# Three modulation groups moved from the last HGRN2 head to heads 3, 5 and 7

## The chip, the cores and the metric

The kernel runs on one core of a Trainium2 chip. The metric is the device time of one execution in microseconds (us); the kernel before takes 1847.86 us, the median of three runs (1847.52 to 1853.19 us). All times inside an execution are counted from its first instruction.

## The reference

The model has two layers over 512 latent and 256 context tokens of width 1024. Each layer is a token mixer and a SwiGLU FFN, and each of the two is fed by an RMS norm that is scaled and shifted by the layer's modulation, and its output is gated by the modulation.

```python
mod_l = jnp.split((jax.nn.silu(c) @ ada_w[i] + ada_b[i])[:, None, :], N_MOD, axis=-1)
...
x = x + mod_l[2] * o_l
x = x + mod_l[5] * swiglu(modulate(rms_norm(x, norm2_w[i]), mod_l[3], mod_l[4]), ...)
```

Layer 0 mixes with latent attention, layer 1 with HGRN2: eight heads, each a gated linear recurrence over the tokens in both directions. `mod[0]` and `mod[1]` (shift and scale of the mixer) are needed before the heads, `mod[2]` when the mixer's output is added to x, and `mod[3]` to `mod[5]` only in the FFN after it.

## The kernel before, in words

**Modulation groups.** The modulation of a layer is a vector of 6144 = 48 x 128 numbers for the two streams. `ada(l, u0, n, ...)` (line 150) computes n = 4 blocks of 128 of it, called a group here and named by its first block u0: four loads of 512 KB (tile `adaw`, line 155), 32 matmuls with two PE instructions each (line 158) into one PSUM bank, a copy on ACT (line 161, tile `rows`), four transposes (line 164) into a second bank and two small operations on DVE (lines 166 and 168). Groups 24, 28 and 32 of layer 1 are a shift and half of a scale for the FFN of layer 1. They read nothing that the heads make.

**The second layer's heads.** `hgrn` loops over h = 0 to 7 (the text counts heads from 1, so head 8 is h = 7). For each head it writes in this order: `head_proj` (projections by the weights HW for two forget gates, q and the output gate: four weight tiles), for every even h the values `iv` of two heads (two weight tiles HWI), `head` (the recurrence: six levels of small matmuls `lv` on PE, each followed by two multiplications on DVE at line 1060, the `grow` step, and a gather `km` on POOL at line 975; then `u`, state updates on DVE, the outputs `o` and the transposes `otp`), and then the modulation groups that a table gives to this head:

```python
for u in ADA_HG[h]:
    with self.at("ada_g"):
        self.ada(1, u, 4, tmp, self.big)
```

After the last head the output projection follows: `out(n)` adds up eight terms, one per head, with one weight tile HWO per n. Five of these sums (three in the three banks `L`, `L`, `M`, two in the bank group that the levels used) can take the terms of the first seven heads while the last head is at work; their eighth terms wait for its result (`o_hi`, line 590). Group 36 comes after these five.

**How a weight gets to PE.** `weight` (line 72) loads 512 KB into a tile `wf` from SP's queue, ACT copies it to a rounded tile `wh` (line 83), and POOL subtracts to get the rest, `wl` (line 84). PE multiplies with both in every term: lines 97, 98 and 99 are the three products. There are four `wf` buffers, and **the loads `adaw` of the groups take the same four** (tag `wf`); `wh` and `wl` have three each. A `wf` buffer that holds a weight is free when POOL has subtracted; one that holds `adaw` is free when PE has done its matmuls.

**What sets the order.** The order on each engine's queue is planned when the program is built: among the instructions that the plan takes to be ready, the one written first goes first, unless a block is marked otherwise. `PRIO` (line 51) moves the recurrences (`hg_head`) 1000 places forward and two kinds of modulation groups of the first layer's part backward (`ada_m`, `ada_n`). `ada_g` is not in it, so a group of `ADA_HG` ranks behind everything that is written before it, the projections and `iv` of its own head among them, and ahead of the next head's projections and their loads. On the chip every queue then runs in that order.

Of the kernel before, what the change touches and what calls it, by code (L numbers as in the profile page):

```python
# [42 lines left out]
RING = 1024  # L43
BT = 3
ADA_HEAD = ((), (16,), (20,), (), (24,), (28,), (32, 36), (48, 52, 56, 60))
ADA_HG = ((), (), (), (), (), (), (), (24, 28, 32))
ADA_O = (36,)
KEEP, CUTS, SB, GSB = (1, 11), (1, 2), (4, 4), (7, 9)
ON_DVE = ((), (0, 1, 2, 3))
# [6 lines left out]
class Kernel:  # L56
# [806 lines left out]
    def hgrn(self, es, a_hi, a_lo, oT):  # L863
# [11 lines left out]
        for h in range(H):  # L875
# [13 lines left out]
            with self.at("hg_head"):  # L889
                self.head(h, ih, pr, oT, tmp, ps, msk, zero, won)  # L890
            for u in ADA_HG[h]:
                with self.at("ada_g"):
# [236 lines left out]
```

## Time and profile before

| what | value |
|---|---|
| median of three runs | 1847.86 us |
| profiled execution, its own time | 1853.65 us |
| its span, first to last instruction | 1851.9 us |
| mean granted TensorE clock | 0.982 |
| PE busy | 1755.5 us, 95% of the span |
| DVE busy | 1016.3 us, 55% |
| ACT busy | 762.6 us, 41% |
| POOL busy | 760.6 us, 41% |
| DMA | 183.61 MB, mean 99 GB/s |

PE is TensorE's matmul side and PEld its weight load, DVE is VectorE, ACT is ScalarE, POOL is GpSimd, and SPq is the queue from which the loads are issued. A row of a timeline gives the start, the duration, the engine, the source line, the operation, out<-in by the program's names, the shape and a count; idle time of the engine just before it stands in brackets with what ended it. The granted clock is 1.00 at TensorE's full clock of 2.4 GHz and 0.50 at 1.2 GHz. A row of windows gives the busy time and, in brackets, the number of instructions of each engine in a stretch. Matmuls overlap in their pipeline, so the step from one row's start to the next tells more than one row's duration.

### The profile page before, as it was taken

The numbers are of one execution on the slowest core, as the hardware profiler recorded it, in microseconds if no ns is written. First come the engines' busy times: TensorE is split into PE (matmuls) and PEld (weight loads), VectorE is DVE, ScalarE is ACT, GpSimd is POOL, SyncE is SP. The second block draws the span as 40 slices with busy tenths as digits, with TensorE's granted clock in tenths as the row PEclk, the third lists the DMA queues.
The fourth block names the chain that finished last, engine by engine and source line by source line (L and its number), as shares of the span: only waits on it lengthen the run. The fifth ranks groups of instructions, "written<-read, shape, count | busy, mean of one in ns | idle before, by whom it ended". The sixth has DMA issues, their size and how long they took to land. (4 is left out here: it accounts for less than half of the span.)

```text
span 1851.9 us, 33106 instructions
## 1 busy us (share of the span) xinstructions
PE 1755.5 (95%) x13708; PEld 1591.8 (86%) x13708; DVE 1016.3 (55%) x1646; ACT 762.6 (41%) x1467; POOL 760.6 (41%) x528
## 2 busy tenths in 40 slices
PE   4889999999899999999999999999998889999999
PEld 3878989788799999988887888888896779999888
DVE  5567887741754445432203666575745278888400
ACT  4355565532554344432213332423333255555411
POOL 2333342216566666643344554554643440000442
PEclk9999999999999999999999999999999989999999
DMA  7412032523222322254224121111115233333331
GB/s 268 137 39 73 25 116 98 170 74 122 103 86 97 104 96 103 81 168 136 86 71 148 60 69 47 61 55 58 58 35 191 94 137 103 103 115 103 108 118 49
DMA packets 55015, 183.61 MB, mean 99 GB/s; under 512 B 6224, under 2 KB 8528, under 8 KB 54864
## 3 DMA queue, kind: packets, MB, share of 16 engines
q1 hardware_dynamic: 53424, 173.62, 28.5%
q10 hardware_dynamic: 1440, 7.86, 1.2%
q8 instruction: 108, 1.77, 0.4%
q14 instruction: 43, 0.35, 0.1%
HBM read 171.50 MB, written 9.96 MB: 98 GB/s over the span
## 5 line engine op out<-in xcount | busy, mean ns | idle before, releaser
L84 POOL TENSOR_TENSOR wl<-wf,wh 128x1024 fp32r<-128x1024 f32 (+2 forms) x130 | 287.0, 2214 | 438.9 <-ACT wh L83 436.5
L83 ACT CAST wh<-wf 128x1024 fp32r<-128x1024 f32 (+2 forms) x130 | 122.9, 947 | 226.2 <-PE L L98 102.5
L97 PE MATMUL q<-op,sh 128*128 128x384 f32 (+1 forms) x640 | 197.3, 310 | 1.0 <-ACT sh L622 1.0
L98 PE MATMUL q<-op,sh 128*128 128x384 f32 (+1 forms) x640 | 197.6, 310 | 0.0
L99 PE MATMUL q<-op,sl 128*128 128x384 f32 (+1 forms) x640 | 194.9, 310 | 0.0
L97 PEld LDWEIGHTS q<-op,sh 128*128 128x128 f32 x640 | 120.3, 188 | 1.5 <-ACT sh L622 1.5
L98 PEld LDWEIGHTS q<-op,sh 128*128 128x128 f32 x640 | 120.3, 188 | 0.0
L99 PEld LDWEIGHTS q<-op,sl 128*128 128x128 f32 x640 | 119.5, 188 | 0.0
L623 POOL TENSOR_TENSOR sl<-wf,sh 128x1024 fp32r<-128x1024 f32 (+1 forms) x40 | 88.7, 2218 | 56.4 <-ACT sh L622 56.4
L98 PE MATMUL L<-op,sh 128*128 128x256 f32 (+1 forms) x360 | 110.4, 307 | 0.0
L99 PE MATMUL L<-op,sl 128*128 128x256 f32 (+1 forms) x360 | 110.3, 306 | 0.0
L97 PE MATMUL L<-op,sh 128*128 128x256 f32 (+1 forms) x360 | 110.3, 306 | 0.0
L1060 DVE TENSOR_TENSOR X<-X,T 128x512 f32<-128x512 f32 x96 | 78.1, 855 | 47.0 <-PE lv L985 45.9
L557 DVE SCALAR_TENSOR_TENSOR xl<-L,mod,xl 128x512 f32<-128x512 f32 x24 | 17.9, 750 | 153.8 <-PE L L99 149.8
L622 ACT CAST sh<-wf 128x1024 fp32r<-128x1024 f32 x80 | 66.7, 834 | 70.2 <-PE L L98 32.7
L98 PE MATMUL L<-f_lo,wh 128*128 128x512 f32 (+1 forms) x240 | 89.1, 371 | 0.0
L97 PE MATMUL L<-f_hi,wh 128*128 128x512 f32 (+1 forms) x240 | 89.0, 371 | 0.0
L99 PE MATMUL L<-f_hi,wl 128*128 128x512 f32 (+1 forms) x240 | 88.5, 369 | 0.0
L158 PE MATMUL L<-adaw,s 128*32 128x128 f32 x1216 | 57.1, 297 | 29.5 <-DMA adaw<-in_ADA 29.3
L975 POOL TENSOR_SCALAR km<-X 128x512 f32<-128x512 f32 x40 | 29.4, 737 | 125.5 <-DVE X L1060 76.4
L622 ACT CAST sh<-sb 128x1024 fp32r<-128x1024 f32 x40 | 42.0, 1050 | 88.5 <-PE q L98 46.6
L158 PEld LDWEIGHTS L<-adaw,s 128*32 128x32 f32 x1216 | 34.8, 116 | 46.1 <-DMA adaw<-in_ADA 17.2
(466 smaller groups left out, 5585.3 us busy)
## 6 DMA issues: line engine op xcount, KB each, us to landing
wf<-in_W SPq DMA_DIRECT2D x104, 512.0 KB, 3.5
adaw<-in_ADA SPq DMA_DIRECT2D x96, 512.0 KB, 4.4
wf<-in_HW SPq DMA_DIRECT2D x32, 512.0 KB, 3.5
wf<-in_W SPq DMA_DIRECT2D x24, 384.0 KB, 3.2
gd<-s SPq DMA_DIRECT2D x10, 768.0 KB, 3.5
g<-gd ACTq DMA_DIRECT2D x10, 768.0 KB, 4.7
wf<-in_W SPq DMA_DIRECT2D x16, 320.0 KB, 3.0
wf<-in_MWO SPq DMA_DIRECT2D x8, 512.0 KB, 4.1
```

Source lines behind the costliest of these rows:

```text
L83: nc.scalar.copy(hi[:, :n], w[:, :n])
L84: nc.gpsimd.tensor_sub(lo[:, :n], w[:, :n], hi[:, :n].bitcast(F32))
L97: nc.tensor.matmul(out, lhsT=lh, rhs=rh, start=(new and i == 0), stop=False, skip_group_check=more)
L98: nc.tensor.matmul(out, lhsT=lh, rhs=rl, start=False, stop=False, skip_group_check=more)
L99: nc.tensor.matmul(out, lhsT=ll, rhs=rh, start=False, stop=(i == n - 1), skip_group_check=more)
L158: nc.tensor.matmul(rows_ps[32 * j:32 * j + 32, i * P:(i + 1) * P], lhsT=self.s32[:, k, :], rhs=w[:, k * P:(k + 1) * P], start=(k < 4), sto ...
L557: nc.vector.scalar_tensor_tensor(xk, po, gate[:, s:s + 1], xk, op0=ALU.mult, op1=ALU.add)
L622: nc.scalar.copy(hi[:, :n], s)
L623: (nc.vector if j in on_dve else nc.gpsimd).tensor_sub(lo[:, :n], s, hi[:, :n].bitcast(F32))
L975: nc.gpsimd.tensor_scalar(km.rearrange("p (m b r) -> p m b r", b=2, r=L), mix, 1.0, 0.0, op0=ALU.mult, op1=ALU.add)
L1060: nc.vector.tensor_tensor(v, v, t, op=ALU.mult)
```

## The change

One table is changed. Group 24 is written after head 3, group 28 after head 5 and group 32 after head 7, where all three stood after head 8. What a group computes and reads stays the same, and so do the number of loads and instructions.

```diff
 ADA_HEAD = ((), (16,), (20,), (), (24,), (28,), (32, 36), (48, 52, 56, 60))
-ADA_HG = ((), (), (), (), (), (), (), (24, 28, 32))
+ADA_HG = ((), (), (24,), (), (28,), (), (32,), ())
 ADA_O = (36,)
```

## Rows read from the trace of the kernel before

**Rows 1.** Windows: busy us of PE, PEld, DVE, ACT, POOL; clock; DMA share, GB/s.
```profile
1150.00:1200.00 50.00, 50.00 (x438) 43.98 (x436) 29.29 (x43) 19.19 (x50) 25.16 (x19) 1.00 0.16 54
1300.00:1350.00 50.00, 47.45 (x546) 41.23 (x546) 32.22 (x39) 14.36 (x32) 27.04 (x20) 0.93 0.17 54
```
**Rows 2.** The same windows over the last head's end.
```profile
1395.60:1421.00 25.40, 18.23 (x446) 14.07 (x449) 16.33 (x27) 10.45 (x24) 6.35 (x7) 0.93 0.72 248
1421.00:1455.70 34.70, 29.96 (x244) 24.47 (x244) 13.18 (x20) 9.62 (x25) 11.13 (x5) 0.95 0.43 138
1407.70:1411.00 3.30, 3.30 (x40) 2.16 (x28) 0.94 (x2) 0.84 (x2) 0.00 (x0) 0.50 1.01 372
```
**Rows 3.** Windows of tile adaw alone: busy us of PE, PEld.
```profile
1395.60:1421.00 25.40, 8.06 (x192) 5.17 (x192) 0.93 0.72 248
1421.00:1455.70 34.70, 2.16 (x64) 1.62 (x64) 0.95 0.43 138
```
**Rows 4.** Windows of tile rows alone: busy us of PE, PEld, ACT.
```profile
1395.60:1421.00 25.40, 1.97 (x12) 1.25 (x12) 1.74 (x3) 0.93 0.72 248
1421.00:1455.70 34.70, 0.60 (x4) 0.47 (x4) 0.59 (x1) 0.95 0.43 138
```
**Rows 5.** Timeline of SP's queue, loads of the second layer's heads.
```profile
1101.67 72.75 SPq L82 DMA_DIRECT2D wf<-in_HW  x8
...
1302.41 26.60 SPq L82 DMA_DIRECT2D wf<-in_HW  x4
1333.80 76.94 SPq L155 DMA_DIRECT2D adaw<-in_ADA  x12
1412.21 3.65 SPq L82 DMA_DIRECT2D wf<-in_HWO  x4
```
**Rows 6.** Waits of SP's queue, 1333 to 1412: us in total, times, longest.
```profile
SPq L155 <- POOL wl L84: 45.4, 4, 27.2
SPq L155 <- PE M L158: 24.9, 3, 20.3
```
**Rows 7.** Timeline of PE from the last projection to the eighth terms.
```profile
1395.32 0.39 PE L99 MATMUL L<-f_hi,wl 128*128 128x512 f32 x1
1395.64 0.84 PE L158 MATMUL M<-adaw,s 128*32 128x128 f32 x18
...
1407.41 0.88 PE L158 MATMUL L<-adaw,s 128*32 128x128 f32 x16 [2.31 <-DMA adaw<-in_ADA]
...
1455.76 0.80 PE L97 MATMUL M<-o_hi,wh 128*128 128x512 f32 x1 [1.49 <-ACT o_hi L590]
```
**Rows 8.** The first weight HWO: timelines of ACT, POOL and PE.
```profile
1416.81 1.05 ACT L83 CAST wh<-wf 128x1024 fp32r<-128x1024 f32 x1 [0.64 <-DMA wf<-in_HWO]
...
1417.93 2.39 POOL L84 TENSOR_TENSOR wl<-wf,wh 128x1024 fp32r<-128x1024 f32 x1 [1.18 <-ACT wh L83]
...
1417.90 0.50 PE L97 MATMUL M<-o_hi,wh 128*128 128x512 f32 x1
```
**Rows 9.** Issue of one load in SP's queue, and the page's loads to landing.
```profile
1396.35 0.33 SPq L155 DMA_DIRECT2D adaw<-in_ADA  x1
...
wf<-in_HW SPq DMA_DIRECT2D x32, 512.0 KB, 3.5
```
**Rows 10.** Timeline of PE where iv ends and the next head's projection begins.
```profile
1159.54 0.40 PE L97 MATMUL M<-f_hi,wh 128*128 128x512 f32 x1
...
1257.97 0.38 PE L1024 MATMUL o<-iv,att 128*128 128x128 f32 x2
...
1260.74 0.46 PE L985 MATMUL lv<-X,km 128*32 128x32 f32 x32
```
**Rows 11.** Timeline of DVE, multiplications of the last head.
```profile
1414.66 1.29 DVE L1060 TENSOR_TENSOR X<-X,T 128x512 f32<-128x512 f32 x2 [1.22 <-PE lv L985]
1417.41 3.46 DVE L1060 TENSOR_TENSOR X<-X,T 128x512 f32<-128x512 f32 x2 [1.46 <-PE lv L985]
...
1421.76 4.69 DVE L1060 TENSOR_TENSOR X<-X,T 128x512 f32<-128x512 f32 x2
```

## The prediction

> **What bounds the kernel now.** I read the page's busy times first, where PE has 95% of the span, and then windows of 50 us over the second layer. Through the middle heads PE is the bound without reserve: it is busy for 50.00 of 50 us from 1150 to 1200 and for 47.45 of 50 from 1300 to 1350, while no other engine passes 33 us [rows 1]. Work that is added there on PE is added to the time. The end of the last head looks different. From 1395.6, when PE has done the last projection [rows 7], to 1421.0 PE is busy for 18.23 of 25.40 us; from there to 1455.7 for 29.96 of 34.70 [rows 2]. At 1455.76 the eighth terms of the output sums start, which need the last head's result [rows 7]. Those 60.1 us are the stage from which the change takes work.
>
> Then I read SP's queue, because the groups share four load buffers with the weights. The twelve loads `adaw` stand right behind the weights of the last head, start at 1333.80 and last for 76.94 us; the first HWO load comes behind them, at 1412.21 [rows 5]. The waits tell why it takes so long: four loads waited for POOL to free a buffer, 45.4 us, and then three waited for PE's matmuls of the first group, 24.9 us, one of them 20.3 us [rows 6]. So the four tiles of group 24 filled all four buffers and lay there; the first was issued at 1333.80 and a load lands in some 3.5 us [rows 9], yet its first matmul ran at 1395.64, directly behind the last projection product at 1395.32 [rows 7]. The planner puts a group behind all that is written before it, however early its data is there, and no weight passes it in SP's queue meanwhile. On this the forecast rests.
>
> **What goes from the last head.** The three groups cost PE 8.06 us for matmuls [rows 3] and 1.97 us for transposes [rows 4], 10.03 us in the 25.4. PE's idle time there is 25.40 - 18.23 = 7.17 us; 2.31 of it in one piece is a group waiting for its own load [rows 7]. PE also lacked other work: the first product with HWO came at 1417.90, as soon as its cast was done, which had waited for the load [rows 8]. With the groups gone the HWO loads follow the last head's weights and are there when the last projection ends, and 3 x 7 terms of the output sums can fill the gaps between the recurrence's levels.
>
> Upper end of the gain: PE's work in the stage without the groups is 18.23 + 29.96 - 10.03 = 38.16 us; a mean clock of 0.95 over the second part means that 3.5 of its 34.7 us ran at half the clock [rows 2], which at full clock is 1.7 less, 36.4; the 34.70 - 29.96 = 4.74 us in which PE waits for the recurrence's last steps [rows 2] stay. That is 41.2 of 60.1 us: 18.9 saved. Lower end: only the 2.31 us wait for a load goes, and the rest of PE's freed time turns into waiting for the recurrence. I take 16, near the upper end, since the row it resembles is the stretch after 1421, where PE has sums to fill with and is busy 29.96 of 34.70 us, idle only in its last steps.
>
> One step of the recurrence bears on this. Two multiplications at line 1060 take 1.29 us at 1414.66, but 3.46 and 4.69 us at 1417.41 and 1421.76 [rows 11], while POOL subtracts HWO weights (one of 2.39 us from 1417.93 [rows 8]). The recurrence loses 2.17 + 3.40 = 5.6 us to that.
> The Trainium skill, page "SBUF — State Buffer", has the rule that VectorE and GpSimd share one pair of ports, held by one of them for a whole instruction, and that a VectorE operation with two SBUF inputs blocks against it. By that rule the collision isn't cured by earlier loads: the subtractions of the two HWO weights that wait for buffers of head 7 still fall into the recurrence, at 2.2 us each, and with 4.4 us less gain the sum below would be +10 in place of +6. The two long rows agree with the rule; whether two of them remain no row shows, and I stay with PE as the bound, for which the recurrence's delay counts only where PE has nothing to fill with.
>
> **What comes into the heads.** A group at full clock costs PE 2.16 + 0.60 = 2.76 us, read from group 36 in the second stretch [rows 3, 4]; three cost 8.3. Its copy on ACT (0.59 us) [rows 4] lies beside PE's work.
>
> The loads move too, all twelve, in three fours, each past the queue of weights. Group 24 is written after head 3, so its loads rank behind `iv` of heads 3 and 4 and ahead of the four weights of head 4, the first of which was issued at 1101.67 [rows 5]. As in the last head, its four tiles will fill the four buffers and lie there until PE has ended `iv`, just before 1159.54 [rows 10]. Behind the waiting load on SP's queue stand head 4's four weights, behind them ACT's cast, POOL's subtraction and PE's projection, which before went on at 1159.54 without a gap [rows 10]. Head 5 and head 7 with groups 28 and 32 have the same pattern.
>
> The first weight's way then lies open to view: 0.71 us from the first matmul of a group to the issue of the next load (1395.64 to 1396.35) [rows 7, 9], 3.5 to land [rows 9], 1.05 for the cast and 2.39 for the subtraction with some 0.3 between them [rows 8], 7.95 us in all; every third product needs the subtraction's result, so PE gets no further before. The group's matmuls lie inside this time. PE can use the rest for recurrence work that is ready. After heads 5 and 7 that is the `o` matmuls of the head before, 1257.97 to 1260.74, 2.77 us [rows 10]; after head 3 no such block stands there, and I count nothing. PE then idles about 4 us after head 3, and 2 to 3 after the others. Idle time of that size has been followed by half clock: behind the 2.31 us gap that ends at 1407.41 [rows 7] the clock stands at 0.50 from 1407.7 to 1411.0 [rows 2]. Such 3.3 us cost 1.65 us of PE time; I count it once in full after head 3 and half of it after heads 5 and 7. Sum: 7.95 + 1.65 = 9.6, and twice 7.95 - 2.77 + 0.83 = 6.0; together 21.6, say 22 us.
>
> Bounds of this: at the low end each tile's matmuls run as it lands and weights never wait, 8.3 us, less the 50 - 47.45 = 2.55 us of idle PE time in two of the stretches [rows 1] if groups fell into it, 3.2 us. At the high end nothing fills: 3 x 9.6 = 29 us.
>
> **The sum.** 22 - 16 = +6 us. The profiled execution took 1853.65 us (span 1851.9 and 1.75 around it), and would take 1859.7. It lies 5.8 us above the median of the runs, near the slowest of the three; on the median 1847.86 the forecast is 1854 us. About 0.3%, 5.5 us, is what a measurement of this kernel can tell from no change, so this is slower by hardly more than that.
>
> **The rivals.**
> *No starvation.* The planner takes a group's matmuls as each tile lands, in small gaps of PE, so the weights keep their lead (head 4's first weight was issued some 58 us ahead of its first product, 1101.67 to 1159.54 [rows 5, 10]). Then only 8.3 us are added and 16 go: -7.7, 1840 us. For it: that lead is large, and the middle heads do have 2.55 us gaps. Against it: a tile issued at 1333.80 [rows 5] lay until 1395.64 [rows 7]. This is the case on the faster side; it decides if fewer than about 2.6 us per group beyond the matmuls are lost.
> *The last head is bound by its recurrence.* The filler is gone, PE waits more, and the stage shortens by 6 instead of 16: +16, 1864 us. For it: the levels run PE, DVE, POOL in turn, and PE's idle at the end was a wait for ACT's `o_hi` [rows 7]. Against it: after 1421 PE is never idle until the last steps [rows 2].
> *Even.* The recurrences of two heads fill the wait after each group nearly whole, the cost is some 16 us, and it balances: 1848 us. For it: PE has boosted recurrence work about; against it: it comes in steps that wait for DVE.
>
> **How the numbers follow.** The forecast gets 0.45, with 1848 to 1861 as its own range; no starvation 0.22, recurrence-bound 0.18, even 0.15. Slower: 0.27 of the forecast's 0.45, the whole 0.18 and 0.01 of the even case, 0.46. Faster: 0.16 of the no-starvation case and 0.01 of the even one, 0.17. Within 0.3%: the rest, 0.37. The range 1840 to 1867 takes in the centres of all the cases and leaves out the far ends of the first two rivals, about 2 in 10.
>
> **What would show it.** In SP's queue: `adaw` in fours ahead of the HW weights of heads 4, 6 and 8, and behind each four a wait of a weight load for PE's line 158 of 20 us or more. On PE: the group directly behind `iv`, then a gap that ends at ACT's or POOL's `wh` or `wl`, and half clock after it. At the end: HWO loads before the last projection has ended, the first `M<-o_hi,wh` some 4 us after it in place of 22, and 41 to 47 us from the last projection to the eighth terms in place of 60. Wrong would be the step of starvation if the weights of heads 4, 6 and 8 are issued before `iv` has ended, and the step of the gain if that last stage stays above 50 us.

## The result and the profile after

The changed kernel takes 1866.87 us, median of six runs (1861.43 to 1871.32), beside 1846.88 for the kernel before: a ratio of 1.0104 (95% interval 1.0082 to 1.0126). A later series of it gave 1865.16 beside 1846.07, 1.0115 (1.009 to 1.014). It is slower by 19 to 20 us, where I had forecast 6. The sign was right and the working was wrong in both of its terms. That the time lies inside my range of 1840 to 1867 us is luck: my forecast's own part of it ended at 1861, and the rest came from a rival.

I cut each trace into the same stages. Boundaries are PE's last product of the first `iv` (heads 1 and 2), its last projection product, and its first eighth term. Two profiled executions of each kernel, in us:

| stage | before | after | difference of the means |
|---|---|---|---|
| start to the end of `iv` of head 1 | 1063.3, 1060.5 | 1067.5, 1064.9 | +4.3 |
| from there to the last projection (the middle) | 332.2, 332.1 | 342.5, 342.4 | +10.3 |
| last projection to the eighth terms (the last stage) | 60.2, 55.7 | 62.7, 60.6 | +3.7 |
| eighth terms to the end | 396.1, 399.3 | 396.8, 396.0 | -1.3 |

In the first stage PE's order is the same in both programs; over all fourteen profiles of this study the stage lies between 1058.3 and 1071.2 us. I take its +4.3 as chance, which two profiles of each can't show. The two spans differ by 17.0 us on the mean; the change shows in the two stages between, with +14. The other 5 to 6 us of the timed difference no stage shows for certain.

One piece of work crosses a boundary of this table. The `o` matmuls of head 7 stand behind the last projection in the kernel before and ahead of it in the changed one:

```profile
1396.41 0.49 PE L1024 MATMUL o<-iv,att 128*128 128x128 f32 x2
```
```profile
1406.20 0.38 PE L1024 MATMUL o<-iv,att 128*128 128x128 f32 x2
...
1408.79 0.48 PE L98 MATMUL L<-f_lo,wh 128*128 128x512 f32 x1
```

They take 2.6 us in the second (1406.20 to 1408.79). With equal work on both sides, the middle grew by 7.7 us and the last stage by 6.3; the sum of the two stays +14.

Windows of the changed kernel: from `iv` of head 3 to that of head 5, on to that of head 7, on to the last projection, the last stage, and one short stretch. The columns are those of [rows 1], with the number of instructions.

```profile
1163.67:1261.12 97.45, 95.10 (x1042) 83.32 (x1040) 59.04 (x82) 32.77 (x75) 50.43 (x38) 1.00 0.23 77
1261.12:1362.46 101.34, 99.25 (x1098) 86.75 (x1096) 63.76 (x84) 34.04 (x83) 52.32 (x38) 1.00 0.23 74
1362.46:1410.03 47.57, 43.40 (x376) 37.97 (x374) 25.53 (x33) 19.16 (x44) 26.97 (x15) 0.93 0.35 116
1410.03:1472.72 62.69, 42.59 (x455) 33.63 (x454) 25.41 (x41) 14.11 (x41) 10.98 (x8) 0.81 0.16 56
1370.70:1377.50 6.80, 4.42 (x27) 3.69 (x28) 3.06 (x5) 3.76 (x6) 4.39 (x2) 0.50 0.52 188
```

The third row answers for most of the middle's cost: 47.57 us, of which PE is idle for 4.2, where the same stretch of before took 36.5 without a gap; 2.6 us of the difference are the `o` products of head 7. The first two rows are no longer than in before (97.7 and 101.8 us), though each holds a group: before had half clock in these two stretches, 3.4 and 6.8 us, and here the clock is 1.00. The fourth is the surprise: the stage that lost 10 us of PE's work is not shorter. [Rows 2] give 48.19 busy of its 60.1 us; here PE is busy for 42.59 of 62.69, idle for 20.1, at a clock of 0.81.

SP's queue after, which answers to [rows 5], and two of its waits:

```profile
1105.80 30.14 SPq L155 DMA_DIRECT2D adaw<-in_ADA  x4
1164.46 20.22 SPq L82 DMA_DIRECT2D wf<-in_HW  x8
...
1310.23 26.16 SPq L155 DMA_DIRECT2D adaw<-in_ADA  x4
1366.71 1.98 SPq L82 DMA_DIRECT2D wf<-in_HW  x4
1375.51 24.79 SPq L82 DMA_DIRECT2D wf<-in_HWO  x5
1405.66 10.27 SPq L155 DMA_DIRECT2D adaw<-in_ADA  x4
```
```profile
SPq L82 <- PE L L158: 58.2, 5, 30.2
SPq L82 <- PE M L158: 28.7, 2, 28.4
```

The loads stand as forecast: groups in fours, and the next head's first weight issued only once PE has begun on the group, after waits of up to 30.2 us. Now PE around the groups, the first one after head 3 and the last one after head 7:

```profile
1163.43 0.28 PE L98 MATMUL L<-wl,f_hi 128*128 128x256 f32 x1
1163.76 0.86 PE L158 MATMUL M<-adaw,s 128*32 128x128 f32 x24
...
1171.67 0.50 PE L99 MATMUL L<-f_hi,wl 128*128 128x512 f32 x1 [1.58 <-POOL wl L84]
...
1362.55 0.41 PE L158 MATMUL L<-adaw,s 128*32 128x128 f32 x4
1362.90 0.49 PE L1024 MATMUL o<-iv,att 128*128 128x128 f32 x2
...
1365.77 0.46 PE L985 MATMUL lv<-X,km 128*32 128x32 f32 x32
1366.06 1.93 PE L158 MATMUL L<-adaw,s 128*32 128x128 f32 x60
1368.66 0.66 PE L164 MATMUL L<-ident,rows 128*128 128x128 f32 x4 [0.41 <-ACT rows L161]
1373.08 0.79 PE L97 MATMUL M<-f_hi,wh 128*128 128x512 f32 x1 [3.76 <-ACT wh L83]
```

Group 24 stands right behind `iv`, and the wait for the first weight leaves one gap of 1.58 us. After group 32 the gap is 3.76 us (1369.32 to 1373.08), and half clock sets in during it: the last window above.

Last, PE in the last stage, to be read with [rows 7], and the POOL and DVE rows beside it:

```profile
1412.21 0.46 PE L985 MATMUL lv<-q,k 128*32 128x32 f32 x32 [2.02 <-ACT q L929]
1416.18 0.65 PE L985 MATMUL lv<-X,km 128*32 128x32 f32 x32 [2.58 <-DVE X L931]
1416.78 0.80 PE L98 MATMUL M<-o_lo,wh 128*128 128x512 f32 x1
...
1427.02 0.39 PE L99 MATMUL L<-o_hi,wl 128*128 128x512 f32 x1
1427.34 0.38 PE L985 MATMUL lv<-X,km 128*32 128x32 f32 x18
...
1441.74 0.66 PE L985 MATMUL lv<-X,km 128*32 128x32 f32 x32 [2.27 <-POOL km L975]
1444.84 0.76 PE L97 MATMUL pl<-o_hi,pw 128*128 128x512 f32 x1 [0.30 <-DVE lm L999]
...
1451.57 0.40 PE L99 MATMUL pl<-o_hi,pw 128*128 128x512 f32 x1
1451.89 0.27 PE L994 MATMUL at<-X 128*64 128x64 f32 x1
...
1472.72 0.79 PE L97 MATMUL M<-o_hi,wh 128*128 128x512 f32 x1 [1.49 <-ACT o_hi L590]
```
```profile
1412.77 2.80 POOL L84 TENSOR_TENSOR wl<-wf,wh 128x1024 fp32r<-128x1024 f32 x1
1419.84 1.65 POOL L975 TENSOR_SCALAR km<-X 128x512 f32<-128x512 f32 x1 [4.26 <-DVE X L1060]
```
```profile
1413.28 2.84 DVE L931 TENSOR_TENSOR X<-q,F 128x512 f32<-128x512 f32 x1
```

POOL has the gather `km` done at 1421.49. The level's matmuls that need it run at 1427.34, 5.85 us later: PE stands in a block of sum products queued ahead of them. Further down it happens again: 21 products `pl` run from 1444.84 to 1451.89, ahead of the 64-wide `at` step. In between PE has no sums left that it can take (the `pl` sum uses the levels' banks and starts only when DVE's `lm` has read them) and waits for DVE and POOL, 2.27 us before a level. The sums are there early, as forecast; they are spent in blocks that hold the recurrence up, and when the recurrence is what everybody waits for, they are gone.

### The profile page after: what moved, and what is told of

It reads as the page before. It is cut to its first block, busy times and chain, and to the rows that moved or that the text cites. A ratio compares the mean times of both kernels' runs of the same rounds, so it can differ in the third digit from the quotient of the medians.

```text
span 1869.5 us, 33108 instructions
## 1 busy us (share of the span) xinstructions
PE 1758.0 (94%) x13708; PEld 1594.1 (85%) x13708; DVE 1015.0 (54%) x1646; ACT 761.5 (41%) x1467; POOL 758.5 (41%) x528
## 5 line engine op out<-in xcount | busy, mean ns | idle before, releaser
L1060 DVE TENSOR_TENSOR X<-X,T 128x512 f32<-128x512 f32 x96 | 72.6, 798 | 61.6 <-PE lv L985 49.9
L97 PE MATMUL L<-gs,wh 128*128 128x512 f32 x180 | 70.7, 394 | 4.2 <-ACT gs L628 4.2
```

The lines of the kernel that those rows point to most:

```text
L97: nc.tensor.matmul(out, lhsT=lh, rhs=rh, start=(new and i == 0), stop=False, skip_group_check=more)
L1060: nc.vector.tensor_tensor(v, v, t, op=ALU.mult)
```

## The experiments

**One group alone after head 7, 24 and 28 in the last head.**
```diff
-ADA_HG = ((), (), (), (), (), (), (), (24, 28, 32))
+ADA_HG = ((), (), (), (), (), (), (32,), (24, 28))
```


> Group 32 alone stands after head 7; groups 24 and 28 stay after head 8. Theory (the time goes where head 8's weights wait for buffers that group 32 holds; the moves after heads 3 and 5 are free): from the end of iv of head 7 to the last projection some 47 us in place of 36.6, with a gap of 3 to 4 us before head 8's first product; whole time +8 to +14 us against the kernel before. Rival (each moved group costs a third of the +20 us): +5 to +8 us. Rival (what is lost is the fill of the last head): the stretch before the last projection grows by the group's own 3 us, and the last stage loses less than with all three gone: +3 to +6 us.

Measured 1857.44 us beside 1848.96, ratio 1.0052 (1.003 to 1.0074), in the theory's +8 to +14. The stretch from head 7's `iv` to the last projection took 44.7 us in place of 36.5, with a gap of 2.04 us before head 8's first product where I expected 3 to 4. Of these 8.2 us group 32's own work is some 2.8, and 2.6 are head 7's `o` products, which stand ahead of the last projection here too. The whole middle took 336.4 us, 4.2 more than before, with 3.4 us of half clock in it where before had 10.2. The last stage stays at 59.2 with one group fewer and without those `o` products.

**The other two alone, 32 in the last head.**
```diff
+ADA_HG = ((), (), (24,), (), (28,), (), (), (32,))
```


> Groups 24 and 28 stand after heads 3 and 5; group 32 stays after head 8. Theory: the two moved groups are free, 97.7 and 101.8 us from iv to iv as before, head 8's weights come in time, and the last stage with one group left takes 55 to 63 us: -5 to +3 us against the kernel before. Rival (each moved group costs a third): +13 us. Rival (fill of the last head lost): +5 to +12 us.

Measured 1857.01 us, ratio 1.004 (1.0018 to 1.0063), 8 us slower where -5 to +3 was expected; the time is that of the rival with the lost fill. The middle took 333.9 us, 1.8 more than before, and the last stage 62.1 in place of a shorter one. So already here the gain was missing.

**No groups at all.**
```diff
+ADA_HG = ((), (), (), (), (), (), (), ())
...
+        nc.gpsimd.memset(self.mod[1][:, 24:36, :], 0.0)
```


> The three groups are left out (their part of the modulation is set to zero), so the heads and the last stage run without them. Theory (the last stage is held by the recurrence, not by PE's work, so 10 us of work less saves nothing): 60 to 64 us from the last projection to the eighth terms, whole time 0 to +4 us against the kernel before. Rival (the prediction's gain of 16 us is there, and only starved weights hide it): 42 to 47 us in that stage, whole time -13 to -18 us.

Measured 1850.23 us, ratio 0.9998 (0.9974 to 1.0023). This is the test of my gain: with 10 us of PE's work taken out of the last stage and put nowhere, nothing is saved. The last stage takes 59.0 us, a little under the expected 60 to 64, PE busy for 42.86 and idle for 16.2:

```profile
1396.33:1455.34 59.01, 42.86 (x480) 34.00 (x478) 27.09 (x42) 15.15 (x43) 10.81 (x9) 0.88 0.20 69
```

In the kernel before, the three groups stood in time that had no better use with the sums queued as they were.

**Six groups of two, after heads 2 to 7.**
```diff
+ADA_HG = ((), (24,), (26,), (28,), (30,), (32,), (34,), ())
...
-                    self.ada(1, u, 4, tmp, self.big)
+                    self.ada(1, u, 2, tmp, self.big)
```


> The same blocks as six groups of two, one after each of heads 2 to 7, so a group can hold two of the four load buffers and never all. Theory (starvation by held buffers): no gap on PE before a head's first product, the first weight of the next head is issued before the group's matmuls; 39 to 41 us from iv of head 7 to the last projection; the last stage as in the changed kernel; whole time +2 to +9 us against the kernel before, 11 to 18 less than the changed one. Rival (groups among the heads cost by their own work and by their banks and copies, six of them more than three): at or above the changed kernel, +18 to +26 us.

Measured 1865.48 us, ratio 1.0101 (1.0051 to 1.0151), as slow as the change. The stretch after head 7's `iv` is 37.3 us without a gap, as the theory had it, but the middle is 342.3 us as in the changed kernel: half-size groups close the gap before head 8, and the cost shows up earlier, in the stretches that end with `iv` of heads 3 and 5 (99.8 and 105.2 us, where the kernel without groups has 96.2 and 97.5). The total lies near the rival's +18 to +26 us (16.5 by the medians, 18.7 by the ratio).

**The sums queued in single terms behind the recurrence.** Here lies the test of why the last stage didn't shorten. Each term of the five sums is tied to a step of the last head's recurrence and can't be queued ahead of it; the work is the same.
```diff
+AFTER = (("lv1", "lv1", "lv1", "lv2", "lv2", "lv2", "lv5", None),
+         ("lv3", "lv3", "lv3", "lv4", "lv4", "lv4", "lv5", None),
+         ("lv5", "lv5", "at32", "at32", "at32", "at64", "at64", None),
+         ("at64", "at64", "u1", "u1", "u1", "u1", "u1", None),
+         ("u0", "u0", "u0", "u0", "o", "o", "o", None))
...
+                            with tc_after(AFTER[n][k]):
+                                nc.tensor.matmul(po[0], lhsT=lh, rhs=rh, start=(k == 0), stop=False)
...
+                    with self.at("ada_o"), tc_after("o"):
```


> The changed kernel, with the five output sums' matmuls queued one term at a time behind named steps of the last head's recurrence (levels, at, u, o), and group 36 behind o; nothing is left out. Theory: in the changed kernel the recurrence of the last head stands in PE's, ACT's and POOL's in-order queues behind whole blocks of sums, which are then used up and leave PE idle (20.1 us). If so the stage from the last projection to the eighth terms falls from 62.7 to 45 to 54 us and the whole by 8 to 17 us against the changed kernel, to 1850 to 1859. Rival: the recurrence's own chain through PE, DVE, POOL and ACT sets the stage whatever PE has beside it; then the stage stays at 58 to 63 us and the time within 4 us of the changed kernel.

Measured 1851.25 us beside 1846.7, ratio 1.0023 (1.0006 to 1.004): 14 to 17 us less than the changed kernel. The last stage, in the columns of the windows above (in the kernels with this edit line numbers are up to 16 higher):

```profile
1401.24:1449.07 47.83, 36.98 (x456) 29.03 (x455) 25.40 (x41) 14.11 (x41) 10.96 (x8) 0.93 0.18 61
```
```profile
1411.04 1.65 POOL L991 TENSOR_SCALAR km<-X 128x512 f32<-128x512 f32 x1 [4.26 <-DVE X L1076]
```
```profile
1412.75 0.48 PE L1001 MATMUL lv<-X,km 128*32 128x32 f32 x32 [0.56 <-POOL km L991]
...
1422.74 0.46 PE L1001 MATMUL lv<-X,km 128*32 128x32 f32 x32
...
1428.78 0.27 PE L1010 MATMUL at<-X 128*64 128x64 f32 x1
...
1449.07 0.50 PE L854 MATMUL M<-o_hi,wh 128*128 128x512 f32 x1 [1.49 <-ACT o_hi L595]
```

The same `km` ends at 1412.69 and its level runs at 1412.75, 0.06 us later in place of 5.85. The last level comes 21.5 us after the last projection (31.7 in the changed kernel), the 64-wide `at` 27.5 us (41.9), the eighth terms 47.8 us (62.7). Nothing in the chain of levels had to get faster; it only had to stop queueing. The edit also puts group 36 behind `o`, but that isn't where the time goes: from the 64-wide `at` to the eighth terms it is 20.3 us here and 20.8 in the changed kernel, so 14.3 of the 14.9 us are saved ahead of it, where group 36 has no part. By the windows, 9.2 us of the 14.9 are less idle time of PE and 5.6 less busy time for the same products, at a clock of 0.93 in place of 0.81. That the low clock followed the waits, and did not itself make the stage long, is argued and not shown. The theory holds, the rival (the chain itself sets 58 to 63 us) falls.

**The same with no groups.** The two edits of the third and fifth experiment together.

> The same queueing of the sums in the kernel in which groups 24, 28 and 32 are left out altogether (set to zero). Theory: last stage 45 to 52 us where it was 59.0 with the sums in blocks, time 1836 to 1843. Rival: last stage 57 to 60 us, time 1847 to 1852 as with the sums in blocks.

Measured 1840.96 us, ratio 0.9963 (0.9939 to 0.9986); last stage 50.2 us in place of 59.0. As expected. It marks about what any placing of the groups can reach with this order of the sums, as long as the rest of the plan stays the same. Beside the last experiment's 47.8 us, this stage holds head 7's `o` products as well.

**The groups ranked forward on PE, loads in the same order.**
```diff
-PRIO = {"hg_head": 1000, "ada_m": -500, "ada_n": -300}
+PRIO = {"hg_head": 1000, "ada_m": -500, "ada_n": -300, "ada_g": 1000}
```


> The changed kernel with the groups ranked 1000 places forward, so that PE takes each of the three some products before the end of iv in place of behind it; the loads keep their order. Theory: the middle cost is 8.3 us of PE work that can't be hidden plus some 5 us of waiting for the next head's weights, so only the second part moves: the 3.8 us gap before head 8's first products shrinks below 2 us and the half clock behind it goes, 3 to 6 us less from the end of iv of head 3 to the last projection, last stage unchanged within 2 us. Rival (the starved weights cost the whole middle, 13.7 us): 8 us or more go.

Measured 1857.35 us, ratio 1.0053 (1.003 to 1.0075), 8 to 11 us less than the change, the rival's size, but not in the middle. From the end of `iv` of head 3 to the last projection it is 5.7 us less (240.6 for 246.3), which hits the expected 3 to 6 by its number alone: 2.7 of it is group 24's work, which now lies ahead of that point, and the other 3.0 are about what head 7's `o` products take, which here stand behind the last projection again. With equal work the middle (339.5 us and these 2.6) is as long as in the change (342.4), although no gap on a weight's cast is left before head 8 and half clock in the middle fell from 6.8 to 3.4 us. The last stage was 58.5 us with the `o` products in it, 2 to 4 less than the change has without them, which the theory hadn't; the rest of the gain lies in no stage that one profile can show. So this run doesn't show that the starved weights by themselves cost the middle anything; how much they do stays open.

**Both kernels again, for a second profile.**

> The kernel before once more, for a second profile of it. Theory: the last stage is 58 to 62 us again and the middle heads 328 to 333 us, so that the stages of one execution can be compared to some 3 us; the time is that of the kernel before within 0.2%. If the last stage comes out at 64 or more, the first profile of it was a lucky one and the gain of the last stage in the changed kernel is larger than it looks.

> The changed kernel once more, for a second profile of it. Theory: last stage 60 to 64 us with 15 us or more of idle PE, middle heads 341 to 344 us, 0.9% to 1.2% slower than the kernel before. If the last stage comes out at 57 or below, the missing gain of the first profile was half chance.

The kernel before measured 1.0005 (0.9986 to 1.0025) against itself, the changed one 1.0115; their stages are in the table at the top. The changed kernel's second profile is as expected, with 19.3 us of idle PE in the last stage. The last stage of before came out 4.5 us shorter than in its first profile, below the 58 that I expected, so that single stages can be compared to no better than that. The 2.31 us wait for a group's load [rows 7] and the half clock behind it [rows 2] belong to the first profile alone; in the second the longest such wait is

```profile
1401.69 0.64 PE L158 MATMUL L<-adaw,s 128*32 128x128 f32 x16 [0.66 <-DMA adaw<-in_ADA]
```

**Three attempts at a faster kernel.** All with the sums queued in single terms, the groups as in the diffs:
```diff
+ADA_HG = ((), (), (), (), (), (), (), (24, 28, 32))
+ADA_HG = ((), (), (24,), (), (28,), (), (), (32,))
+ADA_HG = ((), (), (24,), (), (), (), (), (28, 32))
```


> The kernel before (all three groups in the last head) with the output sums queued one term at a time behind the recurrence's steps, nothing left out. Theory: the sums' blocks held up the recurrence here too, so the last stage falls from 56 to 60 us to 50 to 55, though the weights HWO still come late behind the groups' loads; the middle stays at 332 us; 1840 to 1846 against 1847 for the kernel before. Rival: the last stage of the kernel before is held up by the late HWO loads, not by the queue; it stays at 55 us or more and the time within 3 us of the kernel before.

> Groups 24 and 28 after heads 3 and 5 as in the change, group 32 in the last head, sums queued one term at a time as in e5. Group 32's matmuls fall into the gaps of 2.0 and 3.5 us that PE has at the start of the last stage. Theory: middle 334 to 337 us, last stage 48 to 51, so 6 to 9 us less than e5 (1851.25): 1842 to 1846, faster than the kernel before by 1 to 5 us. Rival: group 32 costs its whole 2.8 us and more in the last stage, 1848 or above.

> Group 24 alone after head 3, where it cost nothing that the stages show, groups 28 and 32 in the last head, sums queued one term at a time. Theory: middle 332 to 334 us, last stage 50 to 53: 1840 to 1845. Rival: with two groups ahead of the sums the HWO weights come late and the sums pile up again, last stage 56 or more, 1847 or above.

Measured, in this order: 1842.08 us, ratio 0.9986 (0.9969 to 1.0002); 1848.73, 1.002 (1.0005 to 1.0034); 1849.13, 1.0018 (1.0003 to 1.0032). The first hit its expectation in the time and with a last stage of 54.7 us, but its interval reaches 1, so that a version faster than both kernels isn't shown. Its rival (late HWO loads hold the stage, at 55 us or more) isn't decided: 0.3 us is less than what two profiles of one kernel differ by. The other two missed; their times are those of the rivals. The second's last stage took 56.1 us, not 48 to 51: with group 32's tiles in the buffers the first HWO load came at 1404.77, after the last projection (1403.97), and head 7's `o` products stand behind the last projection there. In the third, group 24 was not free after head 3: its stage took 101.0 us in place of 97.5 to 97.7, and the last stage 53.7, just over the expected 50 to 53.

## Why the prediction was right in sign and wrong in its working

**Starvation, held in mechanism, mis-sized.** Groups in fours ahead of the HW weights, waits over 20 us behind PE's matmuls, the group right behind `iv`, a gap that ends at `wh` or `wl`: all seen, with half clock at the gap after head 7 alone. The term was 22 us; the middle grew by 10.3 against the kernel before, 7.7 of it with equal work. Against one profile of the same middle code without groups and without half clock (the first of the three attempts, 328.1 us) it is 14.3. That divides into 2.6 of head 7's `o` products, 3.6 more idle time of PE (8.6 us in the windows above, 5.0 there), 2.2 that PE lost in 4.42 us of work at half clock, and 5.9 left for the groups' own work, where I had 8.3. A likely reason, not tested, is that the rows of a tile overlap with their neighbours, so that their busy time is more than they add.

What failed in it is the filling. The way that I had added up to 7.95 us took 7.91 after head 3, from the group's first matmul at 1163.76 to the first product with `wl` at 1171.67, but one gap of 1.58 us was left of it: steps of the recurrence, which I had counted as nothing there, ran in it, and products with `wh`. After head 7 it was the reverse. The `o` matmuls, which I had counted as filler, ran from 1362.90 on, ahead of 60 of the group's 64 matmuls, and these free the buffers. So the next weight was issued at 1366.71, 4.16 us after the group's first matmul, where I had taken 0.71, and 3.76 us of idle time were left.

**The gain in the last head, failed.** This is the step: "3 x 7 terms of the output sums can fill the gaps between the recurrence's levels", and with it 16 of 60.1 us saved. In place of a gain the stage grew, by 2.5 us in the first pair of profiles and by 3.7 on the means, and by 2.6 more than that with equal work. The growth is not far above the 4.5 us by which the two profiles of the kernel before differ; that nothing like 16 us was saved is clear. Its parts came as forecast: HWO loads at 1375.51, before the last projection's end at 1410; the first of the sums some 2.6 us after it in place of 22. And still the eighth terms came at 62.7 us. In that pair PE's busy time fell by only 5.7 us (48.25 to 42.59), though the groups' 10.0 and the `o` products had gone: I had reckoned with full clock, and it was 0.81. Its idle time rose by 8.1 (12.0 to 20.1). I had written that the recurrence's delay counts only where PE has nothing to fill with. The trace shows the opposite direction: the filler itself delays the recurrence, since a queue runs in the order in which it was planned. In the kernel before, PE had no sums during the levels, and the last level ran at 1416.81, 21.3 us after the last projection:

```profile
1416.81 0.46 PE L985 MATMUL lv<-X,km 128*32 128x32 f32 x32 [1.35 <-POOL km L975]
...
1427.88 0.27 PE L994 MATMUL at<-X 128*64 128x64 f32 x1
```

The time was lost behind it, between sums, POOL's subtractions and group 36. With the groups gone the sums moved forward into the levels, and the last level ran at 31.7 us. One delay took the place of the other. Leaving the groups out altogether saved nothing, and queueing the sums in single terms saved 14.9 us of the stage: the first shows that PE's work was not the bound, the second that the order was.

**The rivals.** "No starvation" is out as a mechanism, since the weights were issued behind the groups. In size it was nearer than my term: it added 8.3 us to the middle, and 7.7 were measured with equal work, so that less was lost beyond the matmuls than the 2.6 us per group that I had named as its mark. It fell, as the forecast did, by the 16 us gain, and "even" needed that gain too. The recurrence-bound rival had the nearest time, 1864, by other terms: it let the stage shrink by 6 and took the middle at 22. Its cause is half right, for the recurrence does set the stage, but by its place in the queues; its own chain allows 47.8 us. The lower end of my gain, the 2.31 us wait, rested on an event of one execution.

**The ports.** A multiplication at line 931 takes 0.69 us in the kernel before at 1396.98, with POOL idle, and 2.84 us at 1413.28 in the changed one, with a subtraction of 2.80 us on POOL beside it. Before:

```profile
1396.98 0.69 DVE L931 TENSOR_TENSOR X<-q,F 128x512 f32<-128x512 f32 x1
```

The rule that the prediction weighed (the Trainium skill, page "SBUF — State Buffer", section "Who interferes with whom": a VectorE instruction with two SBUF inputs contends with a GpSimd instruction that reads SBUF) agrees with these rows: earlier loads only moved the collision. It was not the missing gain: the reordered kernel has the same two subtractions at the same place, and its next gather takes 1.65 us too.

## What to carry to other kernels

Idle time of an engine in a stage is not room for gain until you know what the stage's own chain waits for: leave the suspected work out altogether once, and see whether the stage shrinks. Work that "fills gaps" was planned in blocks here, and in a queue that runs in order each block stood ahead of the step that sets the end; tie it in small pieces behind those steps before moving anything away. Work that is moved into a saturated stage is paid for there: two groups, 5.5 us by their rows, added 4.6 us to the middle in two profiles without half clock (332.7 us in the second of the three attempts, 328.1 in the first). And when stages are compared, count first whether the same work lies between the boundaries.

## What I had not expected of the hardware

The half clock does not follow from PE's gaps alone. PE in head 6's recurrence, in the kernel before and in the same kernel with the sums reordered (the first of the three attempts), which have the same gaps here to 0.01 us; the window of each begins 0.78 us ahead of its second row:

```profile
1337.16 0.27 PE L994 MATMUL at<-X 128*64 128x64 f32 x1 [0.98 <-DVE X L1060]
1340.19 0.65 PE L985 MATMUL lv<-X,km 128*32 128x32 f32 x32 [1.57 <-POOL km L975]
```
```profile
1339.41:1346.23 6.82, 6.04 (x57) 5.97 (x58) 1.58 (x4) 0.67 (x2) 1.35 (x2) 0.50 0.01 1
```
```profile
1343.40 0.27 PE L1010 MATMUL at<-X 128*64 128x64 f32 x1 [0.98 <-DVE X L1076]
1346.44 0.46 PE L1001 MATMUL lv<-X,km 128*32 128x32 f32 x32 [1.56 <-POOL km L991]
```
```profile
1345.66:1352.48 6.82, 6.04 (x93) 5.83 (x94) 1.57 (x4) 1.52 (x4) 1.34 (x2) 1.00 0.02 4
```

At 0.50 PE started 57 instructions in 6.82 us, at 1.00 it started 93. In that stage the first took 101.77 us and the other 99.17. The second profile of the kernel before has half clock at the same place:

```profile
1336.31:1343.13 6.82, 5.78 (x57) 5.72 (x57) 1.84 (x4) 0.92 (x3) 1.61 (x2) 0.50 0.00 1
```

So whether it is chance of the execution or belongs to the program, these profiles don't show, and what decides it stays open. Over the middle it amounts to 4.1 us (332.2 with 10.2 us of half clock, 328.1 with none), nearly as much as the 6 us that I had forecast for the whole change.
